# A third couple of row blocks in the seven-product scheme of four projection pairs, with a fused softmax maximum

## The chip, the core and the metric

The kernel runs on one core of a Trainium2 chip. The metric is the device time of one execution, in microseconds (us). Before the change the median of three runs is 2052.86 us (2052.03 to 2053.58). Engines are named as in the profile: PE is TensorE's matmul, PEld its weight load, DVE is VectorE, ACT is ScalarE, POOL is GpSimd, SP is SyncE, which issues most transfers.

## The reference

A trunk of two layers on one sequence of 256 rows of 2048 numbers, all float32:

```python
u = rms_norm(h, a_norm_g); proj = u @ a_w_in          # q, k, v (2048 columns each) and 16 gates
q, k = rms_norm per head (16 heads of 128)
c = cumsum(log_sigmoid(gates + b_f))                  # per head, along the rows
s = q k^T * 128**-0.5 + c[row] - c[column], causal    # layer a
o = softmax(s) v
h = h + o @ a_w_out
h = h + relu(rms_norm(h) @ w1)**2 @ w2                # 8192 wide
kv = rms_norm(h) @ kv_w                               # layer b: own q, chunked attention
...                                                   # with a table of biases, w_out, a second MLP
```

Adding one number to a whole row of s leaves its softmax as it is, so the term c[row] doesn't change the result.

## The kernel before

**Products.** Each float32 matrix product is made of three fp32r passes. A weight tile "raw" is split: ScalarE copies it into hi (rounded), VectorE subtracts hi from it into lo. TensorE then multiplies x_hi by hi (L592), x_lo by hi (L594) and x_hi by lo (L596). hi and lo have three buffers each, so the split of a unit can't begin before TensorE is done with the unit three ahead of it.

**Units and pairs.** A *unit* is a tile of 128 x 1024: two blocks of 128 weight rows by 512 columns. With two blocks of 128 rows of x (b = 0, 1) a plain unit makes 2 x 2 x 3 = 12 matmuls of 512 columns. A *pair* is 1024 output columns, of two halves of 512 (called a and b in the plans), by all 2048 weight rows. In a pair the first weight blocks are not multiplied plainly: two row blocks of x, two row blocks of weights and two column halves form a 2 x 2 block product, and seven products of sums stand for its eight. Such a group of two weight row blocks is a *couple*. The weight side of the seven is the *forms* 11, T3, T2, T1, 21, T4, 22 (form 0 to 6; F in the plans, f0 to f6 in this text): four of them are tiles as loaded, T3 = 22 + 12, T2 = T3 + 11 (VectorE adds, L970, in `make`), T1 = 12 + 11 and T4 = T2 + 21 (accumulating transfers that GpSimd issues, L980, in `put`). The x side comes from sums that VectorE and ScalarE make once (`sums`). The three results are brought together by ScalarE copies and VectorE adds on PSUM (P7, L1020, L995: the *joins*).

Before, the five pairs of the q, k, v projection after the first 1024 columns use two couples each: a form is 128 x 1024, 6 matmuls, and 12 plain units are left. The MLP pairs use four couples ("deep"): a form comes in two parts, the second (`half`) split by itself. One table can also hold three couples (`WIDE`), which before the change nothing uses.

**Order.** `plan` writes out the order of forms and plain units of a pair from a string (F is a form, a4 the fifth plain unit of the first column half). The last three units of a pair (b5 b6 b7) stand between the first forms of the next. `prepare` loads a pair's four form tiles and makes T3 and T1 so many plain units before the pair begins, as a tuple says ("HS", "OFH": for 12, 22, 21, 11, T3, T1). `run` walks the plan; `fetch` and `top_up` split up to three units ahead. Everything else (head norms, attention steps, sums, residuals) waits in a queue of small steps, `fill`; the table HM says how many are run after each unit. The order of each engine's instructions is kept as written.

**Attention of layer a.** For a group of four heads `decay_bias` makes a tile of -c[column] with the causal mask. `softmax` runs per head: scores (L728, L729), then per block of 128 query rows one VectorE instruction that adds c[row] and the bias (L738), one for the negated maximum (L740), then exp, reciprocal, two scalings (L751) and a 32 x 32 transpose (L440). `turn_c` (L902, L903) brings c into rows for L738 by two transposes on TensorE. Layer b has no such term and uses one instruction for sum and maximum (L742).

**Rooms.** Form tiles lie in four buffers k0, k1, v0, v1, beside the keys and values of the running head group. The residual h lies in two tiles of 128 x 2048; x is loaded into it at the start (`rows_in`), read for the row norms, and next touched by the output projection (`residual`).

Of the kernel before, what the change touches and what calls it, by code (L numbers as in the profile page):

```python
# [47 lines left out]
    "OFH": (11, 10, 2, 7, 7, 6),  # L48
# [25 lines left out]
    "XOH": (7, 13, 12, 11),  # L74
# [4 lines left out]
LAZY = ("qkv", "kv", "kv0", "out0", "out1")  # L79
# [20 lines left out]
def trunk(ctx: ExitStack, tc: tile.TileContext, xT, xr, gs, hg, bf, wgate, w_in, w_oa, w1a, w1fa, w1sa, w2fa, w2sa,  # L100
# [63 lines left out]
    class Pair:  # L164
# [3 lines left out]
        def __init__(self, big, src, order, third, units, wide=UN):  # L168
            self.big, self.src, self.third, self.units = big, src, third, units
            self.ps, self.t, self.adds, self.order = None, {}, order != "early", order  # L170
# [90 lines left out]
    def plan_heads(w, when, w_out, rest=None):  # L261
        pairs = []
        for j in range(1 if rest is None else 0, w.shape[0] // 16):
# [4 lines left out]
            pairs[-1].at = 2 * j  # L268
        tail = None
# [9 lines left out]
    plan_h, rest, tail_h = plan_heads(w_in, "H", w_oa)  # L279
# [3 lines left out]
    ready = deque()  # L283
# [21 lines left out]
    def issue(parts=1):  # L305
# [4 lines left out]
        if not cuts:  # L310
# [4 lines left out]
            form.pair.issued.add(form.name)  # L315
# [4 lines left out]
        hi = wsp.tile([P, n], F32R, name="hi" if n == UN else "hih", bufs=3 if n == UN else 1)  # L320
        lo = wsp.tile([P, n], F32R, name="lo" if n == UN else "loh", bufs=3 if n == UN else 1)
# [3 lines left out]
        ready.append((hi, lo, n < UN))  # L325
# [4 lines left out]
        elif form and half == form.pair.wide:  # L330
            if form.name == "T3":
# [4 lines left out]
    def half_next():  # L336
        u = raws[0][0] if raws else units[0]
        return isinstance(u, Form) and u.half and not u.pair.deep
# [353 lines left out]
    def scale_q(land, layer, g):  # L692
        tag = "qs"[g // 2]
# [32 lines left out]
    def softmax(st, g, a, q, k, bias, cq):  # L726
# [9 lines left out]
        for b, c in halves:  # L736
            if cq is not None:
                V.scalar_tensor_tensor(t[:, c], s[:, c], cq[:, b, g * GH + a : g * GH + a + 1], bias[:, a, c],  # L738
                                       op0=ALU.add, op1=ALU.add)
                V.tensor_reduce(nm[:, b : b + 1], t[:, c], axis=AX.X, op=ALU.max, negate=True)  # L740
            else:
                V.tensor_tensor_reduce(out=t[:, c], in0=s[:, c], in1=bias[:, a, c], scale=-1.0, scalar=-3.0 * NEG,  # L742
                                       op0=ALU.add, op1=ALU.min, accum_out=nm[:, b : b + 1])
        yield
        for b, c in halves:
            S.activation(pr[:, c], t[:, c], AF.Exp, bias=nm[:, b : b + 1], scale=1.0 if cq is not None else -1.0,
                         accum_out=su[:, b : b + 1])
# [25 lines left out]
    def attend(g, q, k, v, cq, o, make_bias):  # L773
# [3 lines left out]
        *at, far = TABLES["ATA" if cq else "ATB"][g]  # L777
        items = [[] for _ in range(at[-1] + far + 1)]
        step = steps(lambda: make_bias(g, box))
        for i in (5, 8, 9) if cq and g == 0 else (3, 6, 7):  # L780
# [597 lines left out]
```

## Time and profile before

| what | value |
|---|---|
| median of three runs | 2052.86 us |
| the profiled execution's own time | 2049.66 us |
| its span | 2047.9 us |
| granted TensorE clock | 0.999 |
| PE, PEld | 2041.1 us, 1688.5 us |
| DVE, ACT, POOL | 1783.5 us, 1403.7 us, 245.0 us |

The profile is that of one execution, 3.2 us under the median, so sums made on it are carried over as differences. PE's busy time is modelled from the issue of each matmul and says little on small waits; the starts of the weight loads (PEld) show them. The first q columns take up to 45 us, the five pairs of q, k, v up to about 272 us, the output projection up to about 350, the first MLP follows.

### The profile page before, as it was taken

What the parts mean: (1) busy time and instruction counts of PE and PEld (TensorE: products, weight loads), DVE (VectorE), ACT (ScalarE), POOL (GpSimd) and SP (SyncE); (2) the same over time, 40 slices, a digit from 0 to 9 for tenths busy, and PEclk for the clock granted to TensorE, in tenths of its full rate; (3) what the DMA queues carried; (4) which work ended last, traced back from release to release, by engine and by line L of the source; (5) the groups of instructions that cost most, each with busy time, mean ns of one, the idle gap of its engine ahead of it and who ended that gap; (6) DMA issues with size and microseconds to landing.
All of it is one profiled execution on the core that took longest, in us unless ns stands there. A gap on an engine that the chain in (4) does not pass through costs nothing.

```text
span 2047.9 us, 27097 instructions
## 1 busy us (share of the span) xinstructions
PE 2041.1 (100%) x9062; PEld 1688.5 (82%) x9062; DVE 1783.5 (87%) x2065; ACT 1403.7 (69%) x1805; POOL 245.0 (12%) x351
## 2 busy tenths in 40 slices
PE   9999999999999999999999999999999999999999
PEld 7888888888888888888888888888888888888887
DVE  7788888998898899899988778888988998988996
ACT  7766666677677677677778666667766676776764
POOL 1111110011111102101012111001101111111020
PEclk9999999999999999999999999999999999999999
DMA  8898888998888898898879888888988888888984
GB/s 322 265 298 272 266 280 243 309 278 272 282 262 281 272 293 272 247 292 273 260 242 311 275 254 287 255 264 284 291 291 265 266 270 284 266 284 261 299 259 147
DMA packets 175309, 557.78 MB, mean 272 GB/s; under 512 B 40624, under 2 KB 69184, under 8 KB 152640
## 3 DMA queue, kind: packets, MB, share of 16 engines
q1 hardware_dynamic: 154112, 464.99, 63.9%
q0 software_dynamic: 20768, 90.75, 22.5%
q8 instruction: 71, 1.16, 0.2%
q14 instruction: 70, 0.57, 0.1%
q10 hardware_dynamic: 288, 0.30, 0.1%
HBM read 516.07 MB, written 27.29 MB: 265 GB/s over the span
## 4 chain that ended last, share of the span: by engine, by line
PE 98%; DVE 1%; ACT 1%; issue 0%; DMA 0%; DVEq 0%; ACTq 0%
PE acc L596 23%; PE acc L592 23%; PE acc L594 23%; PE s L592 9%; PE s L594 9%; PE s L596 9%; PE po L729 1%; PE po L766 1%; DVE lo L324 0%; PE po L767 0%; PE po L728 0%; ACT hi L323 0%; DMA gsb<-in_gs 0%; PE pg L868 0%; DVE s L995 0%
## 5 line engine op out<-in xcount | busy, mean ns | idle before, releaser
L324 DVE TENSOR_TENSOR lo<-raw,hi 128x1024 fp32r<-128x1024 f32 (+1 forms) x409 | 493.5, 1211 | 81.5 <-ACT hi L323 77.1
L323 ACT ACTIVATE hi<-raw 128x1024 fp32r<-128x1024 f32 (+1 forms) x409 | 429.5, 1054 | 194.0 <-PE acc L594 123.4
L592 PE MATMUL acc<-hi,act 128*128 128x512 f32 x1774 | 496.3, 393 | 0.7 <-ACT hi L323 0.7
L596 PE MATMUL acc<-lo,act 128*128 128x512 f32 x1774 | 491.1, 390 | 0.7 <-DVE lo L324 0.6
L594 PE MATMUL acc<-hi,act 128*128 128x512 f32 x1774 | 490.7, 389 | 0.0
L596 PEld LDWEIGHTS acc<-lo,act 128*128 128x128 f32 x1774 | 332.5, 188 | 72.1 <-DVE lo L324 3.1
L594 PEld LDWEIGHTS acc<-hi,act 128*128 128x128 f32 x1774 | 333.0, 188 | 70.1 <-DVE act L383 0.5
L592 PEld LDWEIGHTS acc<-hi,act 128*128 128x128 f32 x1774 | 331.2, 188 | 69.6 <-ACT hi L323 2.1
L323 ACT ACTIVATE hi<-w 128x1024 fp32r<-128x1024 f32 x254 | 267.0, 1058 | 124.0 <-PE acc L594 82.7
L324 DVE TENSOR_TENSOR lo<-wT,hi 128x1024 fp32r<-128x1024 f32 x220 | 267.2, 1221 | 66.1 <-ACT hi L323 62.2
L324 DVE TENSOR_TENSOR lo<-w,hi 128x1024 fp32r<-128x1024 f32 x254 | 305.3, 1217 | 14.0 <-ACT hi L323 12.3
L323 ACT ACTIVATE hi<-wT 128x1024 fp32r<-128x1024 f32 x220 | 232.1, 1059 | 102.1 <-PE acc L594 48.5
L592 PE MATMUL s<-hi,act 128*128 128x512 f32 x530 | 146.3, 391 | 0.0
L596 PE MATMUL s<-lo,act 128*128 128x512 f32 x530 | 145.0, 389 | 0.0
L594 PE MATMUL s<-hi,act 128*128 128x512 f32 x530 | 144.8, 388 | 0.0
L466 POOL DMA_DIRECT2D q<-z x192 | 95.7, 510 | 255.1 <-DVE z L440 211.0
L596 PEld LDWEIGHTS s<-lo,act 128*128 128x128 f32 x530 | 99.2, 188 | 20.8 <-DVE lo L324 0.5
L594 PEld LDWEIGHTS s<-hi,act 128*128 128x128 f32 x530 | 99.4, 188 | 20.6
L592 PEld LDWEIGHTS s<-hi,act 128*128 128x128 f32 x530 | 99.1, 188 | 20.2
L592 PE MATMUL s<-hi,S 128*128 128x512 f32 x288 | 89.6, 392 | 0.0
L596 PE MATMUL s<-lo,S 128*128 128x512 f32 x288 | 88.8, 390 | 0.0
L594 PE MATMUL s<-hi,S 128*128 128x512 f32 x288 | 88.7, 389 | 0.0
(217 smaller groups left out, 2284.4 us busy)
## 6 DMA issues: line engine op xcount, KB each, us to landing
raw<-in_w_in SPq DMA_DIRECT2D x75, 512.0 KB, 5.9
w<-in_w2fa SPq DMA_DIRECT2D x32, 1024.0 KB, 6.5
w<-in_w2fb SPq DMA_DIRECT2D x32, 1024.0 KB, 6.2
w<-in_w1fa SPq DMA_DIRECT2D x27, 1024.0 KB, 7.0
w<-in_w1fb SPq DMA_DIRECT2D x27, 1024.0 KB, 7.3
raw<-in_w2sa SPq DMA_DIRECT2D x52, 512.0 KB, 7.0
raw<-in_w2sb SPq DMA_DIRECT2D x50, 512.0 KB, 7.3
raw<-in_w_kv SPq DMA_DIRECT2D x48, 512.0 KB, 5.1
```

Of the source, the lines that this page charges most:

```text
L323: S.activation(hi[:, c], raw[:, c], AF.Copy)
L324: V.tensor_tensor(lo[:, c], raw[:, c], hi[:, c].bitcast(F32), op=ALU.subtract)
L466: (G if i % 2 else SY).dma_start(dst[32 * j : 32 * j + 32, i * n : (i + 1) * n], z[32 * i : 32 * i + 32, j * n : (j + 1) * n])
L592: TE.matmul(ps[:, cols], xh, cut(hi, j), start=first, stop=False, **kw)
L594: TE.matmul(ps[:, cols], xl, cut(hi, j), start=False, stop=False, **kw)
L596: TE.matmul(ps[:, cols], xh, cut(lo, j), start=False, stop=last, **kw)
L729: TE.matmul(s[:, P : 3 * P], q[:, a, P:T], k[:, a], start=True, stop=True)
L766: TE.matmul(po[:, :T], v[:, 0, a * P : (a + 1) * P], pT[:, :2], start=True, stop=False)
```

## The change

1. The last four of the five q, k, v pairs get a third couple (order "three", 1536 columns of forms): a form is now a tile of 6 matmuls and a half of 3, and 10 plain units are left of 12. Their plan is `a3 a4 F a5 F a6 b3 a7 F b4`.
2. The third couple of the form tiles lies in a tile `aside` and in the first 1024 columns of h[0], which hold x by then; these are loaded from x again eight fill steps after the output projection's first pair opens.
3. The sums for the third couple are made by `sum_third`.
4. In these pairs `fetch` splits ahead before each form and each half, as in the deep pairs, not after it; T2 is made after the first part of T3 has been multiplied, not as soon as T3 is split.
5. `make` and `put` do a second, 512-column add or accumulating transfer.
6. The softmax of layer a uses layer b's instruction for sum and maximum; c[row] and `turn_c` are gone.
7. The q tiles of layer a's four groups share one pair of buffers. HM, OFH and the new tuple HT (7, 8, 1, 5, 4, 3) set the times; the output pair's T3 is made 6 plain units ahead, not 7.

TensorE, the first of the four pairs, its T3 and the plain unit behind it (acc and s are PSUM tiles, po scores, R keys and form tiles, S the sums of x). Before:

```order
L592 MATMUL acc<-hi,S 128x512 x2
L594 MATMUL acc<-hi,S 128x512 x2
L596 MATMUL acc<-lo,S 128x512 x2
L592 MATMUL s<-hi,act 128x512 x4
L594 MATMUL s<-hi,act 128x512 x4
L596 MATMUL s<-lo,act 128x512 x4
L728 MATMUL po<-R,q 128x128
L729 MATMUL po<-R,q 128x256
```

The same place after the change:

```order
L607 MATMUL acc<-hi,S 128x512 x2
L609 MATMUL acc<-hi,S 128x512 x2
L611 MATMUL acc<-lo,S 128x512 x2
L607 MATMUL acc<-hi,S 128x512
L609 MATMUL acc<-hi,S 128x512
L611 MATMUL acc<-lo,S 128x512
L607 MATMUL s<-hi,act 128x512 x4
L609 MATMUL s<-hi,act 128x512 x4
L611 MATMUL s<-lo,act 128x512 x4
```

Each form is followed by its half, three matmuls, and the scores now stand elsewhere.

VectorE, near the end of the fifth q, k, v pair, where T3 of the output projection's first pair is made (L970 before, L989 after). Before:

```order
L970 TENSOR_TENSOR wT_2419<-R 128x1024
L324 TENSOR_TENSOR lo<-wT_2117,hi 128x1024
L749 RECIPROCAL row<-row 128x2
L751 TENSOR_SCALAR pbuf<-pbuf,row 128x128
L751 TENSOR_SCALAR pbuf<-pbuf,row 128x256
L440 STREAM_TRANSPOSE pbuf<-pbuf 128x3x4x32
L738 SCALAR_TENSOR_TENSOR t<-po,cq,nb 128x128
L740 TENSOR_REDUCE row<-t 128x1
L738 SCALAR_TENSOR_TENSOR t<-po,cq,nb 128x256
L740 TENSOR_REDUCE row<-t 128x1
L324 TENSOR_TENSOR lo<-raw,hi 128x1024
L771 TENSOR_TENSOR act<-po,act 128x256
```

After the change:

```order
L752 ISA t,row<-po,nb 128x256
L752 ISA row 128x1
L455 STREAM_TRANSPOSE z<-qn 128x4x4x32
L989 TENSOR_TENSOR wT_2493<-R 128x1024
L337 TENSOR_TENSOR lo<-raw,hi 128x1024
L337 TENSOR_TENSOR lo<-wT_2169,hi 128x1024
L337 TENSOR_TENSOR lo<-wT_2169,hi 128x512
L780 TENSOR_TENSOR act<-po,act 128x256
L1163 TENSOR_TENSOR y<-act 128x256 x4
L758 RECIPROCAL row<-row 128x2
L760 TENSOR_SCALAR pbuf<-pbuf,row 128x128
L760 TENSOR_SCALAR pbuf<-pbuf,row 128x256
```

The two maxima instructions per block have become one with a short read of its result, a half stands behind T4's split, and the sums over o and a softmax ending have come close to the add of T3.

The instructions in all: TensorE 12 matmuls of 512 columns and 2 small ones fewer; VectorE 28 half splits, 8 half adds and 10 instructions of `sum_third` more, 8 whole splits fewer; GpSimd 8 accumulating transfers of 256 KB more; SyncE 16 transfers of 256 KB and one of 512 KB more, 8 of 512 KB fewer.

```diff
-    "HM": (1, 2, 1, 0, 0, 1, ...
+    "HM": (1, 2, 1, 0, 0, 1, ...
+    "HT": (7, 8, 1, 5, 4, 3),
-    "OFH": (11, 10, 2, 7, 7, 6),
+    "OFH": (9, 8, 1, 6, 6, 5),
+        ... "three": "a3 a4 F a5 F a6 b3 a7 F b4"},
+    "X3": 10,
...
+            self.steady = self.deep or order == "three"
...
+        if three is not None:
+            f, s = three
+            for i in range(f.shape[0] // 4):
+                src = [[None] * 3 + [s[5 * (2 * i + q) + u] for u in range(5)] for q in range(2)]
+                big = {k: f[4 * i + m] for m, k in enumerate(("11", "12", "21", "22"))}
+                j = len(pairs) + 1
+                pairs.append(Pair(big, src, "three", j % 2 == 1, TABLES["HT" if i else "HS"], WIDE))
...
-                raw = raw[:, UN:]
+                raw = form.pair.e[form.name] if form.pair.e else raw[:, UN:]
...
-            if form.name == "T3":
+            if form.name == "T3" and form.pair.e:
+                second.append(form.pair)
+            elif form.name == "T3":
                 make(form.pair, "T2")
...
-            if cq is not None:
-                V.scalar_tensor_tensor(t[:, c], s[:, c], cq[:, b, g * GH + a : g * GH + a + 1], bias[:, a, c],
-                                       op0=ALU.add, op1=ALU.add)
-                V.tensor_reduce(nm[:, b : b + 1], t[:, c], axis=AX.X, op=ALU.max, negate=True)
-            else:
-                V.tensor_tensor_reduce(out=t[:, c], in0=s[:, c], in1=bias[:, a, c], scale=-1.0, scalar=-3.0 * NEG,
-                                       op0=ALU.add, op1=ALU.min, accum_out=nm[:, b : b + 1])
+            V.tensor_tensor_reduce(out=t[:, c], in0=s[:, c], in1=bias[:, a, c], scale=-1.0, scalar=-3.0 * NEG,
+                                   op0=ALU.add, op1=ALU.min, accum_out=nm[:, b : b + 1])
...
-        def turn_c():
...
+            if p.wide:
+                p.e[name] = beside(p.rooms[name])
+                SY.dma_start(p.e[name], p.big[name][:, UN:])
...
+    def beside(tag):
+        if not aside:
+            aside.extend((qkv.tile([P, UN], F32, name="aside", tag="s", bufs=2), h[0][:, :UN]))
+        i = ("k0", "k1", "v0", "v1").index(tag)
+        return aside[i // 2][:, i % 2 * 512 : i % 2 * 512 + 512]
...
         V.tensor_tensor(d, a, b, op=ALU.add)
+        if e:
+            V.tensor_tensor(*e, op=ALU.add)
...
         G.dma_start(p.t[name][:, cols], p.big[other][:, cols], accum_op=ALU.add)
+        if p.e:
+            G.dma_start(p.e[name], p.big[other][:, UN:], accum_op=ALU.add)
...
-            hi, lo = ready.popleft()[:2] if q > 1 and ready and not p.deep else fetch()
+            hi, lo = ready.popleft()[:2] if q > 1 and ready and not p.steady else fetch()
...
+                if second and q == 2 and u == 1:
+                    make(second.pop(), "T2")
...
-                    if not p.deep:
+                    if not p.steady:
                         top_up(AHEAD - 1)
...
+            if p.order == "out0" and three:
+                add_fill([[]] * 8 + [[lambda: SY.dma_start(h[0][:, :UN], xr[0][:, :UN])]])
```

More of the change, by code (lines that the diff above doesn't have):

```diff
@@ L259, in plan_out, with plan_heads @@
         return plan, [(b, 1, u) for u in (5, 6, 7)]
[L261 removed]
+    def plan_heads(w, when, w_out, rest=None, three=None):
         pairs = []
@@ L314, in issue @@
                 assert form.name + str(int(half)) in form.pair.has, "unit early"
[L315 removed]
+            if half == (form.pair.order == "three"):
+                form.pair.issued.add(form.name)
             raw, cuts = form.pair.t[form.name], [slice(0, form.pair.cols - UN if half else UN)]
             if half:
[L318 removed]
+                raw = form.pair.e[form.name] if form.pair.e else raw[:, UN:]
         n = cuts[-1].stop
[L320 to L321 removed]
+        hi = wsp.tile([P, UN], F32R, name="hi", bufs=3)[:, :n]
+        lo = wsp.tile([P, UN], F32R, name="lo", bufs=3)[:, :n]
         for c in cuts:
@@ L337, in half_next @@
         u = raws[0][0] if raws else units[0]
-        return isinstance(u, Form) and u.half and not u.pair.deep
+        return False
     def top_up(ahead=AHEAD, early=EARLY):
@@ L1197, in heads @@
         base = turns[0]
-        last = next(p for p, q, i in plan_h[::-1] if isinstance(p, Pair) and p.order in LAZY[:2])
-        run(plan_h, opener(x, fs, evacs, o, out, base, last, TABLES["XOH"]), TABLES["HM"], plan_a[0][0])
+        last = next(p for p, q, i in plan_h[::-1] if isinstance(p, Pair) and p.order == "three")
+        step3 = steps(lambda: sum_third(x, fs))
+        add_fill([[]] * TABLES["X3"] + [[step3]] * 4)
+        run(plan_h, opener(x, fs, evacs, o, out, base, last, TABLES["XOH"], True), TABLES["HM"], plan_a[0][0])
         halves_of.clear()
```

71 lines of the change are left out of this document (44 added, 27 removed), and 9 rows, old and new, of the table TABLES.

## The prediction

> **What bounds it.** First the shares and the chain that ended last, then busy time by stretch, then the spacing of TensorE's weight loads, where a wait shows that a busy share hides.
>
> ```profile
> PE 2041.1 (100%) x9062; PEld 1688.5 (82%) x9062; DVE 1783.5 (87%) x2065; ACT 1403.7 (69%) x1805; POOL 245.0 (12%) x351
> PE 98%; DVE 1%; ACT 1%; issue 0%; DMA 0%; DVEq 0%; ACTq 0%
> ```
>
> ```profile
> 45.00:430.00 385.00, 385.00 (x1732) 319.29 (x1732) 327.30 (x458) 257.90 (x412) 53.34 (x60) 1.00 0.86 272
> 430.00:1024.00 594.00, 593.34 (x2615) 490.03 (x2614) 537.75 (x537) 413.24 (x443) 66.11 (x110) 1.00 0.88 275
> 1500.00:2040.00 540.00, 540.00 (x2383) 447.20 (x2382) 479.95 (x469) 361.72 (x375) 58.90 (x98) 1.00 0.85 265
> ```
>
> The columns are stretch, its length, then busy time of PE, PEld, DVE, ACT, POOL, granted clock, DMA share, GB/s. TensorE is the chain (98%) at a full clock. In the third stretch 2383 matmuls of 512 columns fill 540.0 us: 0.2266 us each, and that is the price of a matmul. The changed stage is the first row; DVE is 85% busy there. In the second, at 90.5%, TensorE still idles only 0.66 us.
>
> Loads that stand further apart than 0.2266 us each show all the waiting there is:
>
> ```profile
> 67.05 0.87 PEld L596 LDWEIGHTS acc<-lo,act 128*128 128x128 f32 x4
> 68.27 0.19 PEld L902 LDWEIGHTS pt<-ident,early 16*128 16x128 f32 x2 [0.35 <-issue]
> 68.49 0.30 PEld L592 LDWEIGHTS acc<-hi,act 128*128 128x128 f32 x2
> ...
> 105.33 0.87 PEld L594 LDWEIGHTS acc<-hi,act 128*128 128x128 f32 x4
> 106.47 0.53 PEld L596 LDWEIGHTS acc<-lo,act 128*128 128x128 f32 x3 [0.27 <-DVE lo L324]
> ...
> 355.87 0.76 PEld L592 LDWEIGHTS acc<-hi,act 128*128 128x128 f32 x4 [0.41 <-ACT hi L323]
> ...
> 431.03 0.41 PEld L594 LDWEIGHTS acc<-hi,act 128*128 128x128 f32 x2
> 432.50 0.30 PEld L596 LDWEIGHTS acc<-lo,act 128*128 128x128 f32 x2 [1.05 <-DVE lo L324]
> ...
> 455.85 0.30 PEld L596 LDWEIGHTS acc<-lo,Sh 128*128 128x128 f32 x2 [0.31 <-DVE lo L324]
> ```
>
> Between 70 and 430 us the waits at 105 and 355 us are all there are, under 1 us. So the change can win what it takes off TensorE, and lose what it makes TensorE wait; nothing else counts.
>
> The Trainium skill would read the first row otherwise: "Perfetto Trace Analysis", Identifying the Most-Contended Engine, holds matmul busy time a bad measure and weight-load busy time a good one, which here gives 82% and not 100%. The spacing decides: a load takes 447.20 / 2382 = 0.188 us of each 0.2266 us (83%), so 82% is a full TensorE on 512-column matmuls.
>
> **TensorE, by the orders of both programs.** Each of the four pairs trades two plain units for seven forms' halves: 24 matmuls go, 7 x 3 = 21 come; 3 less, 12 in all: 12 x 0.2266 = -2.72 us. The two transposes of turn_c go. After 67.05 the next unit was due at 67.05 + 4 x 0.2266 = 67.96 and came at 68.49: -0.53 us. Together -3.25 us, all on the path.
>
> **VectorE and ScalarE.**
>
> ```profile
> L324 DVE TENSOR_TENSOR lo<-raw,hi 128x1024 fp32r<-128x1024 f32 x405 | 490.9, 1216 | 80.9 <-ACT hi L323 76.6 <-DMA pbuf<-turn 0.2
> L324 DVE TENSOR_TENSOR lo<-raw,hi 128x512 fp32r<-128x512 f32 x4 | 2.6, 687 | 0.6 <-ACT hi L323 0.5
> L323 ACT ACTIVATE hi<-raw 128x1024 fp32r<-128x1024 f32 x405 | 427.2, 1058 | 193.6 <-PE acc L594 123.4 <-PE s L594 40.3 <-DMA raw<-in_w_in 4.4
> L323 ACT ACTIVATE hi<-raw 128x512 fp32r<-128x512 f32 x4 | 2.3, 623 | 0.3 <-DMA raw<-in_w_in 0.3
> L738 DVE SCALAR_TENSOR_TENSOR t<-po,cq,nb 128x256 f32<-128x256 f32 x16 | 7.6, 475 | 0.0
> L740 DVE TENSOR_REDUCE row<-t 128x1 f32<-128x256 f32 x16 | 6.7, 420 | 0.6
> L742 DVE CUSTOM_DVE_ANT_0 t<-po,rb 128x256 f32<-128x256 f32 x16 | 6.7, 419 | 0.0
> L738 DVE SCALAR_TENSOR_TENSOR t<-po,cq,nb 128x128 f32<-128x128 f32 x16 | 5.4, 338 | 0.5 <-PE po L729 0.5
> L740 DVE TENSOR_REDUCE row<-t 128x1 f32<-128x128 f32 x16 | 4.6, 286 | 0.5
> L742 DVE CUSTOM_DVE_ANT_0 t<-po,rb 128x128 f32<-128x128 f32 x16 | 4.4, 273 | 0.0
> L742 DVE DVE_READ_ACCUMULATOR2_ANT row<- 128x1 f32 x32 | 2.6, 82 | 0.0
> ```
>
> Layer b already runs the fused form (L742), so its price is known: per head 0.475 + 0.420 + 0.338 + 0.286 = 1.52 us become 0.419 + 0.273 + 2 x 0.082 = 0.86; 16 heads save 10.6 us. Each pair adds seven half splits and two half adds, 9 x 0.687, less two splits of 1.216: +3.75 us, x4 = +15.0. The third couple's sums are about +2.5 (ten instructions, from 512 down to 128 columns). DVE: +15.0 + 2.5 - 10.6 = +6.9 us, from 85% to (327.3 + 6.9) / 381.8 = 87.5%. ScalarE: 28 x 0.623 - 8 x 1.058 + 0.6 = +9.6 us, 67% to 70%. On the mean both stay covered by TensorE. What counts is a run of units in which VectorE has more to do than TensorE, since three buffers of hi and lo are all the cover, and a half fills a whole buffer for 0.68 us of TensorE instead of 2.72.
>
> **Where the cover is gone.** VectorE's starts lie closer than its durations, by about 0.08 us:
>
> ```profile
> 1077.77 1.22 DVE L324 TENSOR_TENSOR lo<-R,hi 128x1024 fp32r<-128x1024 f32 x1
> 1078.90 1.21 DVE L324 TENSOR_TENSOR lo<-raw,hi 128x1024 fp32r<-128x1024 f32 x1
> 1080.04 0.69 DVE L995 TENSOR_TENSOR s<-s,p 128x512 f32<-128x512 f32 x1
> ```
>
> ```profile
> L440 DVE STREAM_TRANSPOSE z<-qn 128x512 f32<-128x512 f32 x32 | 22.4, 701 | 4.8 <-ACT qn L674 4.8
> L663 DVE TENSOR_REDUCE ss<-sq 128x4 f32<-128x512 f32 x32 | 21.7, 679 | 2.8 <-ACT sq L660 2.8
> ...
> L440 DVE STREAM_TRANSPOSE pbuf<-pbuf 128x384 f32<-128x384 f32 x32 | 18.5, 579 | 1.1
> ...
> L751 DVE TENSOR_SCALAR pbuf<-pbuf,row 128x256 f32<-128x256 f32 x32 | 11.1, 348 | 0.0
> L751 DVE TENSOR_SCALAR pbuf<-pbuf,row 128x128 f32<-128x128 f32 x32 | 9.2, 287 | 1.1
> ```
>
> So a split costs 1.14 us, a half 0.61, the others their means less as much. In the last of the four pairs, from the end of form T1's first split to the end of a6's, its order holds: six splits 6.84; three half splits 1.83; two joins 1.27; two fused maxima 1.66; two softmax endings (reciprocal, two scalings, transpose) 2.62; two squares' totals 1.68; two turns 1.32; T3 of the output pair 1.14; one attention result and four sums over o 1.95: 20.3 us. Ahead of it are T1's own split and its hi (1.14 + 1.2): 22.65 us since TensorE freed that buffer. TensorE meanwhile has 21.9 us of work: a third of f2 0.45, h2 0.68, b7 and a3 to a5 4 x 2.72, f3 to f5 3 x 1.36, h3 to h5 3 x 0.68, scores for three heads 3 x 0.66, two thirds of a6 1.81. It waits 0.74 us. The same sum for the row at 455.85 is 0.25 us short, and the trace has 0.31; before 430 us the old order is never under 0.9 us to the good.
>
> T2's add has also moved: it now stands right ahead of T2's split, so hi waits for the add, and VectorE has only the half add (0.61) against hi's 1.06 + 0.1: about 0.55 us idle. In the first pair the sum leaves 0.30, in the third 0.45: short by 0.25 and 0.10. New waits: 0.74 + 0.25 + 0.10 = 1.1 us. Bounds: none (the busy mean), and the 1.05 us of row 432.50 at each of the four pairs plus 0.74, 4.9 us; I stay near the sum, since it fitted at 455.85.
>
> **Queues.**
>
> ```profile
> R<-in_w_in SPq DMA_DIRECT2D x20, 512.0 KB, 6.6
> out_h<-h SPq DMA_DIRECT2D x7, 256.0 KB, 5.1
> h<-in_xr SPq DMA_DIRECT2D x4, 512.0 KB, 6.7
> ...
> DMA to landing us min/median/max: 5.1/6.9/10.3
> ```
>
> The loads bring the same bytes in more pieces; 16 pieces of 256 KB join SyncE's queue, eight raw loads leave. GpSimd gets eight accumulating pieces; an issue takes it 0.87 us (row 99.12, below), and the roots queued behind one need nothing sooner than their row totals. New bytes are 2 MB accumulated and 0.5 MB reread, 2.4% of the stage's 105 MB at a DMA share of 0.86. Main loads for T3 are issued three plain units and two forms ahead, 12 us, against 6.6 us to landing: free. The reread waits for its eighth fill step, and its reader, the first residual add, stands some ten units later, over 20 us against 6.7: free. If either cover goes, DVE waits for the landing with every split behind it. "DMA: Bandwidth & Descriptors", Bandwidth, in the Trainium skill gives each transfer 2.0 us fixed and speaks against splitting; by it a 256 KB piece takes an estimated 2.6 us. Landing here is 5.1 us for 256 KB and 6.6 for 512, beneath the lead either way.
>
> **Sum.** -2.72 - 0.53 + 1.1 = -2.15 us. The profiled execution (span 2047.9, time 2049.66) would come to 2047.5; the runs' median, 3.2 us higher, from 2052.86 to 2050.7. What can be told from no change is 0.2%, 4.1 us: the likeliest gain is below that.
>
> **Rivals.** *Full gain* (16%): the new waits stay away and the old ones of this stage (0.9 us) go too: -4.15, 2048.7. For: VectorE has 12% free. Against: the sum at the last pair. *Gain eaten* (20%): every pair loses 1.05 us at its joins: +4.9 - 3.25 = +1.65, 2054.5. For: shorter cover in all four. Against: the second MLP stretch, denser, loses 0.66. *No change* (3%): TensorE isn't the limit, as weight-load busy time would have it; 2052.9. The spacing speaks against it. *Slower* (8%): T4 comes late.
>
> ```profile
> 99.12 0.87 POOL L980 DMA_DIRECT2D wT<-in_w_in  x1 [16.05 <-DVE lo L324]
> ```
>
> ```profile
> 113.66 1.11 ACT L323 ACTIVATE hi<-wT 128x1024 fp32r<-128x1024 f32 x1
> ```
>
> GpSimd's accumulating transfer now waits for T2's half, and has one form half, b7, a3 to a5 and two whole forms until its reader: 15.6 us of TensorE where it had 17.7. The 14.5 us from issue to reader become 12.5, against 5.1 to 10.3 to landing (the row above, 45 to 300 us). From 12.5 on ScalarE stands, with every hi behind it, in all four pairs; at 14.5, 2 us each, +8 - 2.15 = +5.9: 2058.7. The time passes the old one at 0.55 us late each, 0.2% at 1.6.
>
> The likeliest has 53%. Faster by over 0.2% is some two thirds of the full gain, 0.10; slower is the last rival and the tail of the third, 0.09; the rest 0.81. The range takes in full gain and eaten gain: 2048.4 to 2054.6; the likeliest's own is 2049.5 to 2052.
>
> **What would show it.** 12 matmuls of 512 columns fewer, no load of turn_c; a wait of 0.5 to 1 us for DVE's lo near 255 us; L742's kind of price on the new maxima; the end of the stage, where the first MLP pair opens, some 2 us earlier, and after it nothing changed. I am wrong if TensorE waits over 2 us in all between 90 and 300 us, or on an accumulating transfer.

## The result: 16 us slower, and the profile after

The changed kernel takes 2068.66 us (median of 6 runs, 2067.36 to 2070.38) where the kernel before takes 2052.22 (6 runs beside it): a ratio of 1.0079, 95% interval 1.0066 to 1.0092. The forecast was 2050.7 within 2048.4 to 2054.6, so the sign was wrong: 16.4 us lost in place of 2.15 gained.

First the page's busy times and its chain that ended last, then the three stretches that the prediction showed, with the same columns:

```profile
PE 2049.7 (99%) x9048; PEld 1687.1 (82%) x9048; DVE 1786.9 (86%) x2099; ACT 1411.2 (68%) x1826; POOL 253.6 (12%) x359
PE 90%; DVE 3%; issue 3%; DMA 3%; ACT 1%; SPq 0%; POOL 0%; DVEq 0%; ACTq 0%; POOLq 0%
```

```profile
45.00:430.00 385.00, 375.84 (x1657) 306.34 (x1656) 319.10 (x479) 254.35 (x422) 56.52 (x59) 0.99 0.86 269
430.00:1024.00 594.00, 591.66 (x2602) 487.37 (x2601) 534.15 (x530) 409.42 (x434) 70.51 (x118) 1.00 0.88 273
1500.00:2040.00 540.00, 540.00 (x2384) 447.19 (x2383) 485.03 (x475) 369.39 (x384) 62.92 (x106) 1.00 0.87 273
```

The work is what was announced: 9062 - 9048 = 14 matmul records fewer, the twelve and the two transposes. But TensorE is the chain for 90% where it was for 98%, and between 45 and 430 us it gets through 1657 matmuls in place of 1732. VectorE and ScalarE are no busier there than before (83% and 66%): their shares tell nothing of the loss. What TensorE waited for between 45 and 315 us, a list that is empty for the kernel before, in the columns line, releaser, total, times, longest:

```profile
PE s L607 <- ACT hi L336: 3.0, 1, 3.0
PE acc L607 <- ACT acc L1053: 2.0, 2, 1.1
PE acc L607 <- DVE acc L1048: 1.3, 2, 0.6
PE po L743 <- PE acc L611: 0.6, 1, 0.6
PE s L611 <- DVE lo L337: 0.6, 1, 0.6
PE acc L607 <- ACT hi L336: 0.6, 2, 0.4
PE s L607 <- ACT s L1053: 0.5, 1, 0.5
PE acc L611 <- DVE lo L337: 0.2, 1, 0.2
```

Four of the eight rows, 6.1 of 8.8 us, name ScalarE. (Matmul ends are modelled; the weight loads, which the prediction read, show the same waits some 0.4 us longer each.) Two places show the two kinds that most of them are of.

*The first pair, form T2.* VectorE's adds for T2, ScalarE's queue, and TensorE's loads around it:

```profile
97.68 1.22 DVE L989 TENSOR_TENSOR wT<-wT,R 128x1024 f32<-128x1024 f32 x1
98.81 0.68 DVE L991 TENSOR_TENSOR wT<-wT,h 128x512 f32<-128x512 f32 x1
```

```profile
99.01 1.06 ACT L336 ACTIVATE hi<-wT 128x1024 fp32r<-128x1024 f32 x1 [3.97 <-DVE wT L989]
99.98 0.58 ACT L1043 ACTIVATE p<-acc 128x512 f32<-128x512 f32 x1
100.59 0.58 ACT L1053 ACTIVATE acc<-acc 128x512 f32<-128x512 f32 x1
```

```profile
98.84 0.87 PEld L611 LDWEIGHTS s<-lo,act 128*128 128x128 f32 x4
101.22 0.30 PEld L607 LDWEIGHTS acc<-hi,S 128*128 128x128 f32 x2 [1.51 <-ACT acc L1053]
```

The same three instructions of ScalarE before, where the copy p comes first and the split of T2 waits for nothing:

```profile
96.02 0.60 ACT L1015 ACTIVATE p<-acc 128x512 f32<-128x512 f32 x1 [2.70 <-PE acc L596]
96.51 1.05 ACT L323 ACTIVATE hi<-wT 128x1024 fp32r<-128x1024 f32 x1
97.46 0.59 ACT L1025 ACTIVATE acc<-acc 128x512 f32<-128x512 f32 x1
```

After the change the split of T2 was fetched a unit ahead, so it stands on ScalarE in front of the copy p and the scaling of acc, which have nothing to do with T2 but which f2's products need. ScalarE waits 3.97 us, idle, for the add. The order costs more here than the late add: for the split's own reader the add is only 0.3 us late (f2's first load was due at 99.75, the split ends at 100.07), and the wait is 1.47.

*The last pair, behind a7.* ScalarE, TensorE, and the granted clock (the column before the last two):

```profile
275.60 0.38 ACT L779 ACTIVATE act<-po 128x256 fp32r<-128x256 f32 x1 [3.59 <-PE po L776]
276.52 1.15 ACT L417 ACTIVATE S<-sum 128x512 fp32r<-128x512 f32 x2 [0.54 <-DVE row L758]
277.58 1.13 ACT L710 ACTIVATE q<-z,gqk 128x1024 f32<-128x1024 f32 x1
278.62 1.06 ACT L675 ACTIVATE sq<-acc 128x512 f32<-128x512 f32 x2
279.57 1.05 ACT L336 ACTIVATE hi<-raw 128x1024 fp32r<-128x1024 f32 x1
```

```profile
277.02 0.19 PEld L611 LDWEIGHTS s<-lo,S 128*128 128x128 f32 x1
280.67 1.35 PEld L607 LDWEIGHTS s<-hi,act 128*128 128x128 f32 x4 [3.47 <-ACT hi L336]
```

```profile
277.00:280.70 3.70, 0.66 (x4) 0.22 (x2) 2.12 (x5) 3.70 (x7) 0.44 (x1) 0.89 0.32 78
280.70:283.00 2.30, 2.30 (x6) 1.82 (x7) 2.27 (x4) 2.30 (x6) 2.30 (x3) 0.50 0.87 282
285.00:287.00 2.00, 2.00 (x8) 1.56 (x8) 2.00 (x3) 0.00 (x0) 0.00 (x0) 0.57 0.72 128
287.00:289.00 2.00, 2.00 (x11) 1.66 (x10) 0.87 (x3) 1.80 (x6) 0.00 (x0) 1.00 0.62 238
```

The attention step put behind a7 sends the copy of po, two S splits and q to ScalarE's queue ahead of the split of b4 (a head's squares, L675, stand there too). TensorE has f6 and its half meanwhile, 9 x 0.2266 = 2.05 us, then nothing for 3.42. And behind the wait its clock is granted at 0.50: from 280.67 to 286.89 it does in 6.22 us what takes 3.49 at full clock (12 x 0.2266 and the values' 0.77), another 2.73 us.

Read off the loads' spacing, 15 waits of over 0.35 us between 90 and 300 us come to 14.3 us, with the slow stretch to 17.0. Of the 14.3, 7.5 stand at f2 and just behind it in the first, third and fourth of the pairs, and 5.4 behind the last forms' halves and a7 of the third and fourth. Less the 3.25 that the change takes off TensorE, the 17.0 are 13.8. It fits: the same form of the output projection starts at 324.21 us and, before, at 310.55, 13.7 us later. The rest is lost after it, in code that the change leaves alone.

### The profile page after: what moved, and what is told of

Its sections match the earlier page's. It is cut to its first block, busy times and chain, and to the rows that moved or that the text cites. A ratio compares the mean times of both kernels' runs of the same rounds, so it can differ in the third digit from the quotient of the medians.

```text
span 2067.2 us, 27179 instructions
## 1 busy us (share of the span) xinstructions
PE 2049.7 (99%) x9048; PEld 1687.1 (82%) x9048; DVE 1786.9 (86%) x2099; ACT 1411.2 (68%) x1826; POOL 253.6 (12%) x359
## 4 chain that ended last, share of the span: by engine, by line
PE 90%; DVE 3%; issue 3%; DMA 3%; ACT 1%; SPq 0%; POOL 0%; DVEq 0%; ACTq 0%; POOLq 0%
PE acc L611 21%; PE acc L607 21%; PE acc L609 21%; PE s L607 8%; PE s L609 8%; PE s L611 8%; DVE lo L337 2%; DMA q<-turn 1%; ACT hi L336 1%; DMA turn<-z 1%; PE po L775 1%; PE po L744 1%; DMA wT<-in_w1fa 1%; PE po L743 0%; PE po L776 0%
## 5 line engine op out<-in xcount | busy, mean ns | idle before, releaser
L336 ACT ACTIVATE hi<-raw 128x1024 fp32r<-128x1024 f32 (+1 forms) x401 | 420.8, 1054 | 201.0 <-PE acc L609 136.5
L337 DVE TENSOR_TENSOR lo<-raw,hi 128x1024 fp32r<-128x1024 f32 (+1 forms) x401 | 484.4, 1213 | 77.2 <-ACT hi L336 72.4
L337 DVE TENSOR_TENSOR lo<-wT,hi 128x1024 fp32r<-128x1024 f32 (+1 forms) x232 | 274.8, 1193 | 72.3 <-ACT hi L336 66.5
L336 ACT ACTIVATE hi<-wT 128x1024 fp32r<-128x1024 f32 (+1 forms) x232 | 239.2, 1038 | 115.4 <-PE acc L609 46.7
L607 PE MATMUL s<-hi,act 128*128 128x512 f32 (+1 forms) x524 | 146.3, 394 | 3.1 <-ACT hi L336 3.0
L611 PE MATMUL s<-lo,act 128*128 128x512 f32 (+1 forms) x524 | 144.9, 391 | 0.8 <-DVE lo L337 0.6
L609 PE MATMUL s<-hi,act 128*128 128x512 f32 (+1 forms) x524 | 144.4, 390 | 0.0
L607 PE MATMUL s<-hi,S 128*128 128x512 f32 x296 | 92.3, 391 | 0.5 <-ACT s L1053 0.5
L609 PE MATMUL s<-hi,S 128*128 128x512 f32 x296 | 91.8, 389 | 0.0
```

Source lines behind the costliest of these rows:

```text
L336: S.activation(hi[:, c], raw[:, c], AF.Copy)
L337: V.tensor_tensor(lo[:, c], raw[:, c], hi[:, c].bitcast(F32), op=ALU.subtract)
L607: TE.matmul(ps[:, cols], xh, cut(hi, j), start=first, stop=False, **kw)
L609: TE.matmul(ps[:, cols], xl, cut(hi, j), start=False, stop=False, **kw)
L611: TE.matmul(ps[:, cols], xh, cut(lo, j), start=False, stop=last, **kw)
```

## The experiments

Each was timed beside the kernel before, whose median moved between 2050.79 and 2052.17 us; "+12.0" means that much above it. Theories: A, ScalarE's queue has splits fetched early in front of what TensorE needs. B, a half holds a whole unit's buffer, so what is split ahead covers 2 us of TensorE in place of 4. C, the later loss comes from raw loads that take other buffers. D, VectorE has too much work.

### 1. T2's adds early

```
-            if form.name == "T3" and form.pair.e:
-                second.append(form.pair)
-            elif form.name == "T3":
+            if form.name == "T3":
```

> The changed kernel, but T2's two adds are written at once where T3's half is issued, as in the pairs before, and not behind the products of f1. Theory A (ScalarE's queue is in order: the split of T2, written two units ahead, stands there ahead of the copy of p and the scaling of acc that f2's products need, and waits for an add that VectorE reaches late): the first wait of the first pair (1.47 us at 98.8) and those of the same kind in the third and fourth pairs (about 0.9 us each at 195 and 241) go, and some of what follows them at 102 to 106 (2.3 us together); 3 to 5 us less than the changed kernel, 2064 to 2066. Theory B (the waits come from halves that fill a whole buffer, so TensorE's cover ends before ScalarE is through an evacuation): 0 to 1 us less. Theory D (VectorE has too much work in the stage): no gain, since the same adds are done.

Measured: 2069.09 us, ratio 1.0082 (1.0069 to 1.0096), +18.0. No gain in the median. The wait of 1.47 us at f2 did go, but the pair stood again for 2.37 us at 130:

```profile
132.70 1.06 ACT L336 ACTIVATE hi<-raw 128x1024 fp32r<-128x1024 f32 x1 [5.88 <-DMA raw<-in_w_ins]
```

In SyncE's queue that raw load stands behind the probabilities' turn through memory. Against the plain unit that TensorE starts there, it is issued 1.7 us after its first load (127.8 against 126.1), in the third experiment 2.3 us ahead of it (122.2 against 124.5). The turn is late, the load behind it too. That the adds, which now stand ahead of a softmax on VectorE, make the turn late is argued, not shown.

The median hides something here. The profiled execution is 3.6 us behind the kernel before at 25 us already, ahead of the stage: its first products wait 1.75 us, and their loads stand twice as far apart as usual up to 13.3 us. From 25 us to the form of the output projection named above it loses 10.4 us, where the two profiled executions of the changed kernel (the second is the ninth run) lose 13.9 and 13.1. So by the trace the edit is worth some 3 us in the stage, as A expects. Why the median of four executions (2067.07 to 2070.05) shows nothing of it stays open.

### 2. a7 ahead of b3

```
-"three": "a3 a4 F a5 F a6 b3 a7 F b4"
+"three": "a3 a4 F a5 F a6 a7 b3 F b4"
```

> The changed kernel, but in each of the four pairs b3 and a7 change places (a3 a4 F a5 F a6 a7 b3 F b4), their fills with them, so that behind a7 TensorE has a whole unit and a form (4.1 us) and not a form alone (2.05 us) while ScalarE evacuates. Theory B: the 3.42 us at 277 and the 2.15 us of slower loads behind it go, with 0.77 at 212 and 0.61 at 264; 4 to 6 us less than the changed kernel, about 2063. Theory A: the waits at f2 stay, at 98.8 and 102 to 106 (3.8 us), and the one at 277 stays too if its cause is the queue's content and not the cover: 0 to 1 us less. Theory D: nothing is gained.

Measured: 2066.78 us, 1.0072 (1.006 to 1.0085), +15.7. The wait at 277 is still there, 3.53 us:

```profile
275.92 0.39 ACT L776 ACTIVATE act<-po 128x256 fp32r<-128x256 f32 x1 [2.22 <-PE po L773]
279.99 1.07 ACT L333 ACTIVATE hi<-raw 128x1024 fp32r<-128x1024 f32 x1
```

The steps went with their units' places, so the copy of po now stood behind b3, with f6 and its half again as the only cover. The run didn't test B; the fifth does.

### 3. and 10. The buffers' turn, and 9. the changed kernel again

```
-    extra = [False, 0]
+    extra = [False, 8]
```

> The changed kernel, but the count of loaded units, which sends each fifth load of the later layers to another buffer, starts at 8: eight whole units fewer are loaded in the heads, so the loads of all later stages take the buffers again in the order that they had. Theory C (the 3 to 6 us that are lost behind 430 us, in code that the change leaves alone, come from these buffers' shifted turn): 3 to 6 us less than the changed kernel, about 2064; the waits for DMA at 477 and 937 go. Rival (they are spread of single executions, or of the DMA): within 1 us of the changed kernel, and the waits stay or move.

Measured: 2063.10 us, 1.0057 (1.0044 to 1.0069), +12.0. The fifth to seventh kernels, which carry this edit too, stood at +16 to +20, so both kernels were run again on one chip:

> The changed kernel itself, beside the next three on one chip, since the third and the fifth experiment, which differ by one step's place, stood 4 us apart the wrong way round. If runs of one day and chip agree: 2067 to 2070 and a ratio of 1.007 to 1.009 to the kernel before.

> The third experiment's kernel again. Theory C as far as its traces bear it out: the two waits at 937 and 939 us (1.1 to 1.6 us together) stand in all three executions with the shifted turn of the buffers and in none of those with the old turn, and the stretches 430 to 1024 and 1024 to 1500 us hold about 7 and 3 matmuls more with the old turn: 2 to 2.5 us less than the changed kernel. If the 5.5 us of the first time were all this, 5 us less. Rival (nothing but spread): 0 to 1 us less.

Measured: the changed kernel 2068.39 us, 1.0083 (1.007 to 1.0096), +16.9; with the edit 2066.18, 1.0069 (1.0057 to 1.0081), +14.7. So 2.2 us, not 5, with intervals that overlap: the first time was mostly spread, and the reading rests on the trace. What the edit removes is seen in the changed kernel's loads at 937 (ninth run), and in the first MLP stretch of the ninth and of the tenth run:

```profile
937.95 0.30 PEld L607 LDWEIGHTS acc<-hi,act 128*128 128x128 f32 x2 [1.24 <-ACT hi L336]
939.21 0.30 PEld L611 LDWEIGHTS acc<-lo,act 128*128 128x128 f32 x2 [0.49 <-DVE lo L337]
```

```profile
430.00:1024.00 594.00, 590.91 (x2599) 486.90 (x2599) 534.43 (x530) 410.33 (x436) 69.64 (x118) 1.00 0.88 273
430.00:1024.00 594.00, 593.35 (x2615) 490.11 (x2614) 538.03 (x535) 413.28 (x437) 71.64 (x121) 1.00 0.88 274
```

This pair of waits stands in all four executions with the shifted turn (the changed kernel twice, the first two experiments) and in none of the others. It comes to 1.1 to 1.7 us, and for it C holds: eight raw loads fewer shift which loads of later layers take the second buffer. More of the later loss can't be put down to it. By the starts of the same matmuls the changed kernel's two traces lose 5.6 and 5.1 us behind 400 us, but the kernel before with the fused softmax alone (experiments 4 and 15), whose buffers have their old turn, loses 3.3 and 4.0 there against the same trace of before: that much is spread. At 937 ScalarE is idle for 4.55 us until the transfer of w1fa into wT has landed, which GpSimd issued 12 us earlier; how the raw loads' buffers bring that about was not followed further.

### 4. and 15. The fused softmax alone

```
(the kernel before, with)
-            if cq is not None: ... two VectorE passes
+            V.tensor_tensor_reduce(...)      and no turn_c
```

> The kernel before, with the fused softmax in layer a alone and without the turned decay column (two transposes and a copy); pairs, orders and tables as before. From the prediction's terms: 0.5 us for the transposes and up to 1 us for waits behind VectorE, so 2051 to 2052, within 0.2% of before. Theory D, or any theory in which the fused form itself holds up TensorE through the waits of its exponentials: 2054 or more.

> The fourth experiment's kernel again (the kernel before with the fused softmax alone), to settle its sign: 2049.68 against 2051.06, with an interval of 0.9984 to 1.0002. From the transposes that go and the 10 us of VectorE's time: 0.5 to 1.5 us less than before; if it was spread, equal within 0.5 us.

Measured: 2049.68 us, 0.9993 (0.9984 to 1.0002), -1.4; again: 2051.75, 0.9995 (0.9986 to 1.0004), -0.4. VectorE's busy time between 45 and 315 us falls by 10.2 us, as the prediction had it, and TensorE has nearly nothing of it: its loads stand 0.6 and 0.4 us earlier at 311 us, about the two transposes. The second time is within the 0.5 us that stood for "equal". This part does no harm; a gain is not shown.

### 5. The step behind f6 instead of a7, last pair

```
 HM, last pair:   a7 1 -> 0,  f6 0 -> 1      (with the edit of 3)
```

> The third experiment's kernel (the buffers in their old turn) with one more edit: in the last of the four pairs the step of attention work that stood behind a7 stands behind f6. Theory B, mended after the second experiment (there the step came behind b3, with f6 and h6 again as TensorE's only cover, so that run did not test it): the copy of po sits at the head of ScalarE's queue and waits 3.6 us for TensorE to reach the values, and the split of b4, the S splits and the scaling of q stand behind it. Moved behind f6, the split of b4 gets ahead of them: the wait of 3.43 us goes, and with it the 2.7 us that the stretch of halved clock behind it costs, if the halved clock follows from the wait. 5 to 6 us less than the third experiment's 2063, about 2057 to 2058. Rival (the split of b4 waits for the buffer that the half holds, whatever stands in the queue): 0 to 2 us less, the wait stays above 2 us.

Measured: 2067.07 us, 1.0079 (1.0062 to 1.0097), +16.3. No gain in the time, though the wait is gone as B says, and the clock stays at 1.00 over 277 to 300 us. ScalarE has the split of b4 ahead of the copy now:

```profile
278.86 1.06 ACT L333 ACTIVATE hi<-raw 128x1024 fp32r<-128x1024 f32 x1
281.04 0.39 ACT L776 ACTIVATE act<-po 128x256 fp32r<-128x256 f32 x1 [0.17 <-PE po L773]
```

```profile
302.63 0.30 PEld L740 LDWEIGHTS po<-R,q 128*128 128x128 f32 x2 [1.93 <-issue]
```

Between 197 and 296 us TensorE gains 3.9 us on the third experiment's execution, and by 350 it loses 1.8 again: being earlier, it waits for the turned k. The rest went in waits ahead of the edit, where the two programs are alike and this execution falls 3.9 us behind (2.1 us before the scores at 159, 1.0 at 49). That the halved clock follows from the wait is shown; that the edit pays is not, in this kernel.

### 6. No fetching ahead

```
-            self.steady = self.deep or order == "three"
+            self.steady = self.deep                     (with the edit of 3)
```

> The third experiment's kernel with the four pairs' forms and halves not fetching a unit ahead of their products: as in the kernel before, they take what is ready and top up behind the products. Theory A: the copy of p and the scaling of acc then stand ahead of the split of T2, and the waits for the scaling (1.47 us at 98.9, 0.84 at 241) go: 1.5 to 3 us less than the third experiment's 2063, about 2061. Rival E (fetching first was what made room for the halves, which hold a buffer for 0.7 us of work): more waits for ScalarE's and VectorE's splits at the forms, 2065 or more.

Measured: 2069.03 us, 1.0085 (1.0069 to 1.0102), +18.2: rival E. The scaling no longer makes TensorE wait, as A says. But now p stands ahead of the split that TensorE needs next:

```profile
191.92 0.60 ACT L1043 ACTIVATE p<-acc 128x512 f32<-128x512 f32 x1 [3.70 <-PE acc L611]
192.41 1.05 ACT L336 ACTIVATE hi<-raw 128x1024 fp32r<-128x1024 f32 x1
```

```profile
193.51 0.53 PEld L607 LDWEIGHTS s<-hi,act 128*128 128x128 f32 x3 [2.05 <-ACT hi L336]
```

Twice 2.05 us (the other at 241). By the times alone the step is less sure: the interval overlaps that of the third experiment's second time. Either order on that queue loses something while two buffers ahead are one form and one half.

### 7. The old softmax

```
 softmax as before the change, turn_c back          (with the edit of 3)
```

> The third experiment's kernel with layer a's softmax in its old form (two VectorE passes per half, the turned decay column and its two transposes), so that VectorE gets 10.6 us more work between 45 and 290 us. Theory D (VectorE's load makes TensorE wait there): at least half of it shows, 2068 or more. Theories A and B (ScalarE's order of work makes TensorE wait): the transposes' 0.5 us and up to 2 us for exponentials that start 0.6 us later, 2063.5 to 2065.5.

Measured: 2070.71 us, 1.0095 (1.008 to 1.011), +19.9, that is 5 to 8 us over the same kernel with the fused one. The expectation under D was met, under A and B not. The same places wait longer (the scaling at f2: 3.5 us in all, against 2.0; VectorE's lo 1.9 over two rows, against 1.0 in the third experiment), and the longest of them, 2.33 us, is followed by a stretch at half clock that the third experiment's trace doesn't have there. So D holds in part: with the halves' short cover, VectorE's extra time reaches TensorE; in the kernel before (experiment 4) the same 10 us didn't.

### 8. Fetching first alone

```
+            self.steady = self.deep or order == "qkv"     (the kernel before, plain units)
```

> The kernel before with one part of the change alone: in layer a's attention pairs with all twelve matmuls to a unit, each form fetches a unit ahead of its products and tops up nothing behind them. Theory A as the cause by itself (a split fetched early stands ahead of the copy of p and the scaling): a wait of about 1 us at f2 of each of these pairs, 2055 to 2060. If it takes the halves and the late T2 as well, as theory B would have it: within 1.5 us of before, 2050 to 2052.5.

Measured: 2052.69 us, 1.0010 (1.0000 to 1.0020), +1.9. No wait over 0.41 us between 67 and 430 us in its trace, so by the trace the second case; the time, just over the 1.5 us allowed there, leaves a small cost open. Fetching ahead alone doesn't bring the wait at f2; it takes the late T2 as well (experiment 1). Whether it also takes the halves no run separates.

### 11. and 12. Buffers of their own for the halves

```
-        hi = wsp.tile([P, UN], F32R, name="hi", bufs=3)[:, :n]
+        hi = wsp.tile([P, n], F32R, name="hi" if n == UN else "hih", bufs=3 if n == UN else 1)
...
-        ready.append((hi, lo, False))
+        ready.append((hi, lo, n < UN))
```

> The third experiment's kernel with T2's adds written early, and with buffers of their own for the halves' splits (one each of 128x512 for hi and lo), which then no longer count among the units held ahead; room for them comes from one working buffer (5 to 4) and the small tiles' buffers (6 to 3). Theory B (a half holds a whole unit's buffer, so the splits ahead of TensorE last 2.05 us where they lasted 4): nearly all waits for ScalarE's and VectorE's splits behind halves go, 6 us or more less than the next kernel, which has all but the halves' buffers. Rival D (VectorE and ScalarE have too much work there, wherever it is put): 0 to 3 us less.

> The third experiment's kernel with T2's adds written early and with the room taken away that the experiment before this gives to the halves (one working buffer fewer, three small tiles' buffers fewer), and nothing put in its place: the measure for that one. From the first and third experiments 2063 to 2067; if the working buffers themselves are needed, more, up to 2070.

Measured on one chip: 2061.33 us, 1.0049 (1.0036 to 1.0063), +9.8, with the buffers; 2066.70, 1.0075 (1.0063 to 1.0087), +15.2, with the room taken and nothing put there. The buffers are worth 5.4 us by the medians, with intervals that meet, a little short of B's 6 and above D's 3. What TensorE still waits for with them:

```profile
PE po L741 <- DMA R<-turn: 3.2, 2, 1.9
PE po L773 <- DMA pbuf<-turn: 2.5, 1, 2.5
PE acc L605 <- DVE acc L1046: 2.0, 2, 1.1
PE acc L609 <- DVE lo L337: 1.0, 1, 1.0
PE s L605 <- ACT hi L336: 0.6, 1, 0.6
```

ScalarE's splits are down to 0.6 us, from 3.6 in the changed kernel and 7.1 with the room taken. First stands a wait that the changed kernel hardly had: data turned through memory.

The Trainium skill ("Perfetto Trace Analysis", Optimization Strategy) takes a gap that repeats on the engine that should be full as a hint that the next tile has no buffer. The trace agrees: nearly all of the repeated waits behind halves went with two buffers of 128x512.

### 13. and 14. The sixth and the fifth edit again, now with the buffers

```
 13: the edits of 11 and of 6;    14: those and the edit of 5
```

> The eleventh experiment's kernel (buffers of their own for the halves), and the forms do not fetch ahead of their products, as in the sixth. Theories A and B together: the sixth experiment showed that without fetching first the waits at f2 go (3.7 us in the first pair) and come back as splits that are late behind halves (2 x 2.0 us); with buffers for the halves the second cannot happen. So 2 to 4 us less than the eleventh experiment's 2061.3, about 2058. If the two are one and the same shortage, moved about (rival F: VectorE's and ScalarE's work between the forms is too much in any order): 2061 or more.

> The kernel before this one with the step of attention work moved from a7 to behind f6 in the last pair, as in the fifth experiment. Theory B with its own cause removed by the buffers: nothing more to gain from the step's place, within 1 us of the kernel before this one, or 1 to 2 us worse by the round trip of the next turn through memory, which starts later (the fifth experiment's wait of 1.9 us at 300).

Measured: 2061.25 us, 1.0040 (1.0027 to 1.0052), +9.1, and 2057.75, 1.0025 (1.0016 to 1.0033), +5.6. In 13 the wait for the scaling at f2 is gone in the first and fourth pairs, and the two of 2 us that this edit cost in the sixth are not there: by the trace A and B are two causes. The time is the one that rival F named: it hardly moves, as the turned data take part of what was won (6.6 us of waits for them in its trace, 5.7 in the eleventh's), and this execution lost 2.4 us at 86 to a raw load that came late (0.9 at that place in the eleventh). 14 is 3.5 us faster than 13, against the expectation, with intervals that overlap. What is left in 14, but for two rows of 0.3 and 0.2 us for VectorE's lo:

```profile
PE po L738 <- DMA R<-turn: 2.4, 1, 2.4
PE po L738 <- issue: 1.7, 1, 1.7
```

### 16. The scores one step later

```
-    "ATA": (..., (9, 12, 15, 18, 12), ..., (9, 9, 12, 12, 9)),
+    "ATA": (..., (10, 12, 15, 18, 12), ..., (10, 10, 12, 12, 9)),
```

> The fourteenth experiment's kernel (buffers for the halves, no fetching ahead, the last pair's step behind f6), and the first scores of the second and fourth group of heads come one step later: 10 where 9 stood in two rows of the table of attention steps. Its only waits over 0.75 us before 315 us are two in which the scores wait for the turned k (2.79 us at 154, 2.07 at 290), whose read from memory starts 8 us ahead of them where the kernel before has 12.5. If a step (a unit, 2.7 us) covers that: 4 to 5 us less than the fourteenth experiment's 2057.8, about 2053, within 0.2% of the kernel before. If the later scores make the probabilities late by as much: no gain, 2057 to 2059, the waits now at the values.

Measured: 2053.55 us, 1.0012 (1.0003 to 1.0021), +2.5. The turned k is waited for no more; all that TensorE waits for between 45 and 315 us:

```profile
PE acc L602 <- ACT hi L333: 0.3, 1, 0.3
PE s L606 <- DVE lo L334: 0.3, 1, 0.3
PE acc L606 <- DVE lo L334: 0.2, 1, 0.2
```

From +16.9 to +2.5 on the way 9, 10, 12, 11, 13, 14, 16: +16.9, +14.7, +15.2, +9.8, +9.1, +5.6, +2.5. By the loads' spacing six waits of 0.43 to 0.69 us are left in the stage, 3.4 us, and they eat the 3.25: at 311 us the same matmul stands 0.2 us later than in the kernel before. The +2.5 comes in small pieces behind it: 1.0 us by 328 us, where two waits of 0.43 us stand for ScalarE's copy of the attention's values, 1.7 in all by 1024, 2.8 at the end. What brings the later ones is open; the pools made smaller for the buffers may have a part in it, and so may spread. No version here is shown to beat the kernel before.

## Why the prediction was wrong, point by point

- **Matmuls and transposes, -3.25:** 14 records fewer, as said. Not disputed by any run.
- **The step that failed: "both stay covered", and with it the term of 1.1 us for new waits.** 14.3 us of waits and 2.7 us at half clock were measured in its place. VectorE and ScalarE were costed by their mean share, and then VectorE's order was summed over runs of units, ScalarE's not at all. Most of the loss is on ScalarE's queue. The sentence "hi waits for the add, and VectorE has only the half add (0.61) against hi's 1.06 + 0.1: about 0.55 us idle" looked at who idles and not at who is queued behind: p and the scaling of acc stood behind that hi, TensorE behind them, and ScalarE idled 3.97 us, since the add itself stood behind a softmax's ending, two maxima and a split. TensorE lost 3.8 us (1.47, 0.39, 1.01 and 0.90) at f2 and just behind it in the first pair, where 0.25 was summed.
- **The cover.** The prediction says that a half fills a whole buffer for 0.68 us of TensorE, but it drew the sum from that for VectorE alone. What two buffers ahead are worth to ScalarE when one of them is a half was left at nothing: 2.05 us in place of 4.1 at a7's evacuation. Experiments 11 and 12 price that at 5.4 us.
- **The 0.74 us at the last pair:** a wait for VectorE's lo stands there, 0.62 us at 267, at the unit that the sum named, a6. VectorE's order sum came near; that ScalarE's hi is 0.61 us late for the same unit was not in it.
- **Softmax, -10.6 us of VectorE, and its price per head:** right (10.2 measured alone, 0.42 and 0.28 us per maximum). That this would not show alone: right. That the changed kernel has VectorE time to spare: wrong (experiment 7).
- **Queues "free":** the new 256 KB loads landed after 5.1 and 5.8 us, as summed. T4's accumulating transfer made TensorE wait nowhere in the stage; its new 256 KB pieces landed after 6.9 us. The slowest new pieces, those of T1, took 10.6 and 11.5 us, over the 10.3 that the prediction had as the most, with no wait behind them. No run showed the reread late. But transfers that the change doesn't touch lost cover: k's read from memory starts 12.5 us ahead of its scores in the kernel before, at 155, and 7.6 ahead in the changed one, at 159, with 0.98 us of waiting in it; in experiment 14 it is 8.0 with 2.75 of waiting. That row was never looked at. (The 2.0 us fixed, which the prediction cites from the Trainium skill, stand in "DMA: Bandwidth & Descriptors" under Anatomy of one DMA, for transfers issued by GpSimd; the sum didn't use them.)
- **"After it nothing changed":** wrong, by 1.1 to 1.7 us of waits in the traces and 2.2 in the medians. Fewer raw loads shift a count that steers later buffers; the counter stood in the code to be read.
- **The rivals:** "gain eaten" had the direction, and at f2 the place as well, since p and the scaling belong to the joins; it allowed 1.05 us a pair, and the first pair alone lost 3.8. The slower rival was the wrong mechanism. The test set for being wrong, over 2 us of waits between 90 and 300 us, came out at 14.3.

## What to carry to other kernels

Sum the order on every in-order engine that feeds the busy one, not only on the one with the highest share, and ask of each early instruction what stands behind it. A buffer that holds a smaller unit is a shorter lead: count leads in time of the consumer, not in buffers. Where several engines are near their limit, one wait taken away shows the next one, so a single undo can read as no gain; take them away one upon the other.

## What the hardware showed that was not expected

TensorE's granted clock halves after a single wait, and the stretch at 0.50 has one of two lengths: 6.83 us in three of the fourteen such stretches ahead of the last 10 us of the runs' traces (the changed kernel, the sixth run, the tenth at 285), 3.41 in the other eleven. It can begin up to 1.3 us behind the wait's end. In the changed kernel 6.83 us, part of them in the wait itself, add 2.7 us; in the first and third runs the same wait of 3.42 us has 3.41 behind it. The clock also fell behind 2.33 us (seventh run), 2.61 (twelfth) and 2.83 (eleventh), but stayed at 1.00 behind 2.33 (first), 2.40 (thirteenth) and 2.75 (fourteenth). So here a wait of 2.3 to 2.8 us may or may not cost it.

The Trainium skill ("TensorE: Matmul & The Clock Gate", Part 1: The HAM clock gate) gives half rate after about one idle window of 3.4 us, and a window that runs freely. The half rate agrees, and so does 3.41 us as a length; the wait that it takes doesn't quite, since 2.33 us was enough once.

Executions of one program spread by some 6 us, the kernel before too (2049.17 to 2055.27 in the 15 runs beside experiments 1 to 4). In three of the profiled executions TensorE stood 3.0, 2.7 and 2.5 us for a raw load that came late, near 88 us in the tenth, 231 in the twelfth and 87 in the thirteenth, in the first two with the clock lowered behind it. Differences of 2 to 4 us between neighbouring experiments lie within overlapping intervals, and rest on the traces beside them.
